# One bank pool, two operand buffers and wider products for a bidirectional recurrence

## The chip, the cores and the metric

The kernel runs on one core of a Trainium2 chip, in one launch. The metric is the device time of one execution in microseconds (us). Everything is computed in 32-bit floats. A 32-bit matrix product appears in the profile as two matmul records and two weight loads.

## The reference, cut to what matters

One layer with two parallel recurrent branches is followed by a mixture of experts. There are 256 context tokens and 256 latent tokens of width 1024.

```
u   = rmsnorm(h) * (1 + scale1) + shift1            # h: context, latent
p   = u @ w_in                                       # 6032 columns
yA  = gated_delta_net(p[A cols])                     # 4 heads x 128, chunks of 64, two directions
yB  = rwkv7(p[B cols])                               # 8 heads x 64, two directions
      # S_t = S_{t-1} (diag(w_t) + a_t b_t^T) + v_t k_t^T ;  y_t = S_t r_t
h  += gate1 * w_out(sig(p[gA]) * yA @ w_oA + sig(p[gB]) * yB @ w_oB)
h  += gate2 * moe(rmsnorm(h) * (1 + scale2) + shift2)    # 32 experts, two of them per token
out = rmsnorm(h)                                     # latent tokens only
```

Context tokens are needed for the recurrent states alone. The latent tokens of both branches start from the states that the context left.

## The kernel before

**Front.** `make_u` and `ada_first` compute the modulated input, which stays in SBUF as `u`. `proj` multiplies one 128-column tile of `w_in` with it: eight products of 128x128 weights into a PSUM tile `pj`, over 512 tokens (both streams) or over the 256 latent tokens. Most of TensorE's time goes there. `gate_cols` does the sixteen tiles of the two output gates and, after every second one, a piece of the modulation weights (`ada_rest`). These gate tiles need nothing but `u`, so they serve as filler.

**RWKV branch.** `rwkv_prep` makes the decayed operands of one segment (0 context, 1 latent) and one head pair p, sends them to DRAM (`rscr`), and computes the within-chunk products `ab` in the PSUM tile `abps`. `inverse` inverts the chunks' triangular matrices column by column on DVE (the pairs `itm`, `ixt`), and `inverse_join` joins the 32x32 halves on TensorE (`zps`). Then come four context steps (`R`) and four latent steps (`r`) of `rwkv_step`. One step loads X and A from DRAM (`rX`, `rA`), transposes the scaled keys (POOL `rKE`, PE `tmps`, ACT `rtm`) and the values (`vps`, `ruv`), makes the within-chunk products `akps` and masks them into `rak` and `rbk` (DVE), forms the right side `rps`, solves with the inverse (`ups`), updates the state (`sps`, `sbd`), and in a latent step writes the output (`yps`).

**GDN branch.** `gdn_cols`, `gdn_v`, `gdn_kk` and `gdn_kq` prepare keys, queries and values, a second `inverse` follows, and `gdn_step` runs eight steps: `gkt`, `gvt`, `gks`, `gup`, `gsp`, and for latent steps `gop` and `got`. `rwkv_post` and `merge_b`, `gdn_post` and `merge_a`, `out_rows` and `route` follow, then eight quads of four experts (`moe_quad`) that stream 100 MB of weights through six `wgu` and seven `wd` slots.

**Memory.** PSUM has eight banks of 128x512, dealt out by tag in `PSB` (L97): pp 1, sc 2 (one tile that spans both), pj 1, gc 2, ch 2. `sc` holds `abps`, `tmps`, `akps`, the joins' `zps` (except the last) and three tiles of `rwkv_post`; only one of these lives at a time. X has one buffer (`NB["rX"]`), so a step's load of X is issued after the last product of the step before has read it.

**Order.** The program is written as straight-line code. A planner simulates the engines and writes one fixed order of instructions for each engine and for each DMA queue: among the instructions that are ready by its own clock it takes the one of highest precedence. Precedence is the order of writing; `high_priority(n)` (in `hi`, L1517) moves a block n instructions ahead. In the string `go` of `NB` the parts between the two recurrences are written as `KGGgGGRRGRRikIVGQqJrrrrG`: K, Q, V are projections of the GDN branch, G a gate tile, R and r the recurrence steps, i and I inverses, J a join. R, i, I and J have 2000, V has -400, r has none. On the chip each engine executes its list strictly in order; SyncE (SP) issues nearly all DMAs, also in order. A pool (`w2`, twelve weight buffers) opens after the last latent step, in the space of the recurrence's operands, and the eight last gate tiles load through it.

Of the kernel before, what the change touches and what calls it, by code (L numbers as in the profile page):

```python
# [52 lines left out]
def constants():  # L53
# [21 lines left out]
    for d in range(2):  # L75
        mr[:, d] = (np.where(half == d, -1.0, 1.0)[:, None] * incl)[:, None]
# [20 lines left out]
PSB = {"pp": (1, 512), "sc": (1, 1024), "pj": (1, 512), "gc": (2, 512), "ch": (2, 512), "mx": (4, 512)}  # L97


class K:  # L100
# [64 lines left out]
    def psum(self, tag, name="ps"):  # L165
        b, w = PSB[tag]
        return (self.ps2 if tag in ("sc", "ch") else self.ps).tile([P, w], F32, tag=tag, bufs=b, name=name)
# [289 lines left out]
    def rwkv_prep(self, seg, p, B, ab, pool):  # L457
# [69 lines left out]
        m = self.cst("mka").unsqueeze(1).to_broadcast([P, 8, C])  # L527
        ps = self.psum("sc", name="abps")
        pv = ps.rearrange("p (e s j n) -> p e s j n", e=2, s=4, j=2)
        for e in range(2):  # L530
            r = slice(64 * e, 64 * e + 64)
            for s in range(4):
                for j in range(2):
                    for d in range(2):
                        self.mm(pv[64 * d:64 * d + 64, e, s, j, :], bks[d][r, s, j, d, :], acs[d][r, s, j, 0, :])
        for e in range(2):
            for s in range(4):
                self.tt(abv[:, e, s, 2 * p:2 * p + 2], pv[:, e, s], m[:, 0:2])
# [65 lines left out]
    def rwkv_step(self, seg, s, T):  # L604
        nc = self.nc
        x = lambda name, *dims, bufs=2: self.t(self.prt, name, *dims, bufs=bufs)
        X, A = self.t(self.prx, "rX", 1536, bufs=NB["rX"]), self.t(self.prx, "rA", 512 + 512 * seg, w=1024, bufs=2)
# [10 lines left out]
        if upd:  # L618
            KE = self.t(self.prx, "rKE", 2, 4, P, bufs=1)
            self.tt(KE, X[:, 0:1024].rearrange("p (d j n) -> p d j n", d=2, j=4), pc.to_broadcast([P, 2, 4, P]),  # L620
                    eng=nc.gpsimd)
            ps = self.psum("sc", name="tmps")
            for d in range(2):
                for j in range(4):
                    self.tr(ps[:, (4 * d + j) * P:(4 * d + j + 1) * P], KE[:, d, j])
            for d in range(2):
                self.act(tm[:, d, :], ps[:, d * 512:d * 512 + 512], scale=self.cst("sgn")[:, d:d + 1])
            if S is not None:
                Sp = self.t(self.pst, "rS", 2, 4, C, bufs=1)
# [9 lines left out]
        ak, rbk = x("rak", 2, 4, C), None  # L639
        if seg:  # L640
            rbk = [self.t(self.prx, "rbk", 2, 2, 2, C, bufs=NB["rbk"]) for _ in range(2)]
        for p in range(2):
            ps = self.psum("sc", name="akps")
            pv = ps.rearrange("p (e x) -> p e x", e=2)
            for e in range(2):
                r = slice(64 * e, 64 * e + 64)
                for j in range(2):
                    for d in range(2):
                        ko, uo = 64 * (1 - d), 64 * d
                        bk, a = BK[r, d, 2 * p + j], AR[r, d, 2 * p + j]  # L650
                        self.mm(pv[ko:ko + 64, e, j * C:(j + 1) * C], bk[:, 1 - d, :], a[:, 0, :])
                        if seg:
                            c0 = 128 + (2 * d + j) * C
                            self.mm(pv[ko:ko + 64, e, c0:c0 + C], bk[:, 1 - d, :], a[:, 1, :])
                            self.mm(pv[uo:uo + 64, e, c0:c0 + C], bk[:, d, :], a[:, 1, :])
            for e in range(2):
                self.tt(ak[:, e, 2 * p:2 * p + 2, :], pv[:, e, 0:128].rearrange("p (j n) -> p j n", n=C),
                        self.cst("mks").unsqueeze(1).to_broadcast([P, 2, C]))
            if seg:
                self.tt(rbk[p].rearrange("p e d j n -> p e (d j n)"), pv[:, :, 128:384],  # L660
                        self.cst("mkr").unsqueeze(1).to_broadcast([P, 2, 256]))
# [3 lines left out]
        for h in range(8):  # L665
            e, j = h % 2, h // 2
            for d in range(2):
                ur, kr = slice(64 * d, 64 * d + 64), slice(64 * (1 - d), 64 * (1 - d) + 64)
                self.mm(rv[ur, h, :], ak[kr, e, j, :], uv[kr, d, h * C:(h + 1) * C], start=S is None or h == 0,
                        stop=S is None)  # L670
# [31 lines left out]
        if seg:  # L702
            yp = self.psum("ch", name="yps")
            yv = yp.rearrange("p (d j n) -> p d j n", d=2, j=4)
            for h in range(8):
                e, j = h % 2, h // 2
                r = slice(64 * e, 64 * e + 64)
                for d in range(2):
                    o = yv[r, d, j, :]
                    self.mm(o, Sb[:, d, j, 64 * e:64 * e + 64], AR[:, d, j, 1, :], start=True, stop=False)  # L710
                    self.mm(o, uv[:, d, h * C:(h + 1) * C], rbk[j // 2][:, e, d, j % 2, :], start=False, stop=True)
# [9 lines left out]
    def rwkv_post(self, pool):  # L721
# [7 lines left out]
        for tgt in range(2):  # L729
            ps = self.psum("sc", name="mean")  # L730
            for i in range(2):
                self.mm(ps[:, i * 512:(i + 1) * 512], self.cst("bd"), f(yc if tgt else self.RY)[:, i * 512:(i + 1) * 512]
                        if tgt == 0 else f(sq)[:, i * 512:(i + 1) * 512])
            if tgt == 0:
                self.stt(f(yc), ps, -1.0 / 64, f(self.RY), ALU.mult, ALU.add)
                self.act(sq, yc, AF.Square)
            else:
                self.rsq(f(sq), ps, 64.0, 1)
# [3 lines left out]
        ps = self.psum("sc", name="gate")  # L742
        for j in range(4):
            self.mm(ps[:, j * L:(j + 1) * L], g2[:, j * P:(j + 1) * P], self.Bg)
        self.tt(yc, yc, ps.rearrange("p (j n) -> p j n", j=4))
# [229 lines left out]
    def gdn_step(self, s, T, tmp):  # L975
# [16 lines left out]
        ps = self.psum("pp", name="gvt")  # L992
# [36 lines left out]
        if lat:  # L1029
# [12 lines left out]
            ps = self.psum("pp", name="got")  # L1042
# [397 lines left out]
NB = {'st': 2, 'ys': 'PP', 'yc': [1, 1], 'hn': 'VAVA', 'im': 'AAPP', 'e': 7, 'rt': 13, 'w': 10, 'e1': 4, 'o2': 2, 'kvr': 2, 'cv': 'PVVPPVPPPVVV', 'g1': 3, 'g2': 0, 'imt': 1, 'gi': 0, 'hi': {'p00': 2500, 'p01': 2500, 'i0': 2500, 'gp': 2000, 'R': 2000, 'i': 2000, 'gs': 2000, 'I': 2000, 'J': 2000, 'p11': 200, 'j0': 1500, 'g': 400, 'V': -400, 'rw': 2000}, 'zf': 1, 'g0': 1, 'pe': 0, 'vr': 'vr', 'jt': 'pp', 'go': 'KGGgGGRRGRRikIVGQqJrrrrG', 'rX': 1, 'rbk': 2, 'ixt': 1, 'vh': 2, 'bk': 4, 'ar': 3, 'gm': 7, 'fp': [[28, 'pj'], [29, 'gc'], [20, 'gc'], [21, 'ch'], [22, 'ch']], 'at': ['pp', 'sc'], 'pf': {'ma': 2, 'oo': 0.5}, 'pm': 8, 'aa': 1, 'gr': 0, 'gu': ['pj', 'gc', 'gc'], 'gq': 2, 'gk': 2, 'w2': 12, 'ip': [0, 0, 4], 'gt': ['pj']}  # L1440
# [72 lines left out]
def build(tc, A, dbg=None, upto="all"):  # L1513
# [6 lines left out]
    with ExitStack() as ctx:  # L1520
# [7 lines left out]
        with ExitStack() as mix:  # L1528
# [4 lines left out]
            with ExitStack() as ph1:  # L1533
# [6 lines left out]
                with ExitStack() as s:  # L1540
# [27 lines left out]
                    with hi("j0"):  # L1568
                        k.inverse_join(ab[0], pinv, T0, t0, "sc")
# [24 lines left out]
                def inv1():  # L1594
                    t[1] = k.t(mp, "iT", 32, C)
                    x = k.inverse(ab[1], pinv, t[1], 1)
                    k.inverse_join(ab[1], pinv, t[1], x, "sc")
# [82 lines left out]
            for n, c, tag in (("gp", k.MID, "sc"), ("gq", k.OUT, "gc")):  # L1680
# [66 lines left out]
```

## Time and profile before

| | us |
|---|---|
| median of 3 runs | 889.32 (887.65 to 893.66) |
| the profiled execution | 891.71 |
| its span, first to last instruction | 889.9 |
| TensorE busy | 774.4 (87% of the span) |
| VectorE busy | 389.6 (44%) |
| mean granted TensorE clock | 0.917 of full speed |
| HBM read | 189.64 MB |

The span is what the trace covers; 1.8 us of the execution lie around it. PE is TensorE's matmuls, PEld its weight loads, DVE VectorE, ACT ScalarE, POOL GpSimd, SP SyncE. A granted clock of 1.0 is 2.4 GHz and 0.5 is 1.2 GHz; a value between them is a mean over a stretch. Busy time of matmuls is the union of records whose ends overlap the next one's start, so it is a guide to occupation and not to efficiency. The profile has one row per group of instructions with its busy time, its mean duration and the idle time in front of it. The rows used are quoted below.

### The profile page before, as it was taken

To read this page: it belongs to the slowest core of one execution; us is meant where nothing else is said; L and a number is where in the kernel's file an instruction comes from. 1 tells how busy PE (TensorE), PEld (TensorE's weight loads), DVE (VectorE), ACT (ScalarE), POOL (GpSimd) and SP (SyncE) were. 2 spreads that over 40 slices of the span, in tenths; PEclk is the share of its full clock that TensorE was granted. 3 is DMA by queue.
4 is the path that set the end of the run, shared out by engine and by line. 5 is a ranking of instruction groups with operands and counts; after the bars stand their busy time and mean duration, and the time that the engine had idled before them with its cause. 6 is when DMAs were issued, how large, how long until landed. Compare 5 with 4: busy or idle time off the path is not lost. (4 is left out here: it accounts for less than half of the span.)

```text
span 889.9 us, 15079 instructions
## 1 busy us (share of the span) xinstructions
PE 774.4 (87%) x6089; PEld 460.2 (52%) x6089; DVE 389.6 (44%) x799; ACT 228.7 (26%) x434; POOL 192.9 (22%) x279
## 2 busy tenths in 40 slices
PE   6999999896948899989889999969969996888785
PEld 1444657542535575576677766758445441333231
DVE  1324679999499343895234512233162210111012
ACT  0323554313544233246412231150030000000001
POOL 1013335355243153762401110000120000000000
PEclk8999899798868999999769999998989998899988
DMA  9831454454322963465463399987974999999993
GB/s 347 304 101 64 127 183 160 165 161 131 116 81 77 303 202 125 126 183 158 154 209 96 91 359 316 304 271 229 330 309 176 431 423 426 422 428 425 426 410 119
DMA packets 88361, 210.60 MB, mean 237 GB/s; under 512 B 7753, under 2 KB 37201, under 8 KB 80865
## 3 DMA queue, kind: packets, MB, share of 16 engines
q1 hardware_dynamic: 85248, 205.87, 63.7%
q10 hardware_dynamic: 3040, 3.74, 1.2%
q8 instruction: 49, 0.80, 0.4%
q14 instruction: 24, 0.19, 0.1%
HBM read 189.64 MB, written 19.94 MB: 235 GB/s over the span
## 5 line engine op out<-in xcount | busy, mean ns | idle before, releaser
L106 PE MATMUL pj<-u,w 128*128 128x256 f32 (+1 forms) x768 | 253.0, 484 | 5.5 <-DVE gz L119 2.6
L106 PEld LDWEIGHTS pj<-u,w 128*128 128x128 f32 x768 | 148.1, 198 | 96.7 <-issue 72.1
L106 PE MATMUL gup<-wgu,xs 128*32 128x512 f32 x512 | 79.1, 687 | 22.4 <-DMA wgu<-in_wgu_dram 22.3
L106 PEld LDWEIGHTS gup<-wgu,xs 128*32 128x32 f32 x512 | 19.9, 124 | 77.6 <-issue 45.6
L112 DVE TENSOR_TENSOR msg<-msg,gup 128x256 f32<-128x256 f32 x8 | 3.4, 422 | 120.8 <-ACT msg L122 120.8
L112 POOL TENSOR_TENSOR rl<-rl,mhalf 128x1 f32<-128x1 f32 x2 | 1.1, 548 | 226.7 <-DVE rl L116 226.7
L112 DVE TENSOR_TENSOR itm<-ixt,imt 128x31 f32<-128x31 f32 (+22 forms) x89 | 44.8, 503 | 4.3 <-POOL ixt L551 2.3
L106 PE MATMUL dnp<-wd,mhT 128*32 128x512 f32 x256 | 38.6, 598 | 4.1 <-DVE mhT L1343 4.1
L112 DVE TENSOR_TENSOR ixt<-ixt,itm 128x31 f32<-128x31 f32 (+22 forms) x89 | 40.8, 459 | 2.2
L122 ACT ACT_TABLE_LOAD x24 | 30.8, 1283 | 30.0 <-PE kkn L106 12.7
L106 PEld LDWEIGHTS xsp<-oh,h 128*128 128x128 f32 x256 | 32.6, 203 | 6.2 <-issue 6.2
L106 PE MATMUL xsp<-oh,h 128*128 128x128 f32 x256 | 34.0, 287 | 0.0
L112 POOL TENSOR_TENSOR cacc<-cacc,cm 128x512 f32<-128x512 f32 (+1 forms) x24 | 26.5, 1103 | 26.4 <-ACT cm L122 25.3
L122 ACT ACTIVATE msg<-gup 128x256 f32<-128x256 f32 x8 | 3.1, 383 | 112.4 <-PE gup L106 112.4
L106 PE MATMUL acc<-my,ohT 128*128 128x512 f32 x64 | 29.7, 596 | 0.0
L106 PE MATMUL acc<-w,m 128*128 128x512 f32 x64 | 28.3, 592 | 0.0
L122 ACT ACTIVATE xs<-xsp 128x512 f32<-128x512 f32 x8 | 4.8, 597 | 91.3 <-PE xsp L106 91.3
L112 POOL TENSOR_TENSOR shs<-xp 128x512 f32<-128x512 f32 (+1 forms) x15 | 13.4, 896 | 64.3 <-ACT xp L122 64.3
L112 POOL TENSOR_TENSOR h<-xres,rowscale 128x512 f32<-128x512 f32 x4 | 5.1, 1271 | 100.6 <-DVE xres L112 100.6
L112 POOL TENSOR_TENSOR gS<-gS,sdec 128x1024 f32<-128x1024 f32 x6 | 11.5, 1912 | 68.6 <-PE gop L106 39.7
L116 DVE TENSOR_SCALAR shtm<-pj,omu 128x256 f32<-128x256 f32 x25 | 12.0, 481 | 29.6 <-ACT xp L122 29.6
L106 PE MATMUL akps<-rA,rX 64*64 64x64 f32 x512 | 23.5, 245 | 1.4 <-ACT rtm L122 1.4
(374 smaller groups left out, 1265.4 us busy)
## 6 DMA issues: line engine op xcount, KB each, us to landing
wgu<-in_wgu_dram SPq DMA_DIRECT2D x28, 2048.0 KB
wd<-in_wd_dram SPq DMA_DIRECT2D x27, 1024.0 KB
w<-in_w_in_dram SPq DMA_DIRECT2D x96, 256.0 KB
w<-in_ada_w_dram SPq DMA_DIRECT2D x64, 256.0 KB
aw<-in_ada_w_dram SPq DMA_DIRECT2D x16, 512.0 KB
rX<-rscr SPq DMA_DIRECT2D x8, 768.0 KB
wgu<-in_wgu_dram SPq DMA_DIRECT2D x20, 256.0 KB
rscr<-bk SPq DMA_DIRECT2D x8, 512.0 KB
```

The source lines that it names most:

```text
L106: return self.nc.tensor.matmul(out, lhsT, rhs, start=start, stop=stop)
L112: (eng or self.nc.vector).tensor_tensor(out=out, in0=a, in1=b, op=op)
L116: (eng or self.nc.vector).tensor_scalar(out=out, in0=a, scalar1=s1, scalar2=s2, op0=op0, **kw)
L122: return self.nc.scalar.activation(out=out, in_=in_, func=func, **kw)
```

## The change

PSUM loses the tag `sc`. Its two banks go to `ch`, which now has four single banks for all these tiles; `gvt` and `got` of the GDN step move from `pp` to `ch` as well.

In `rwkv_prep` the `abps` products are written so that consecutive ones use the upper and lower half of the rows (e, in two banks) and both halves of the columns (d), and each bank is masked by one 128x512 operation in place of four of 128x128.

In a context step the sixteen products of both head pairs go into two banks and are masked by two operations in place of four. In a latent step a product takes both operands whole: 64 rows, 128 columns of weights, 128 moving columns. It replaces three of 64 by 64 (half of its upper output is not used), so 16 products stand for 48, and four masks of 128x512 stand for four of 128x128 and two of 128x512. The masked operands take eight buffers of 2 KB per partition (`arb`). X gets two buffers. Both together need 14 KB per partition more, net of `rak` and `rbk`. `rwkv_post` works in two halves.

The table of precedences gets `'r': 1000`: each latent step moves 1000 instructions ahead of where it is written, which is further than V, G, Q, q and J together are long. I and J keep their 2000. Nothing else of `NB` changes but the bank tag of `adat` (`'at'`: `['pp', 'ch']`).

```
     mr = np.zeros((P, 2, 2, 64))
     for d in range(2):
-        mr[:, d] = (np.where(half == d, -1.0, 1.0)[:, None] * incl)[:, None]
+        mr[:, d, 0] = strict
+        mr[:, d, 1] = np.where(half == d, -1.0, 1.0)[:, None] * incl
...
-PSB = {"pp": (1, 512), "sc": (1, 1024), "pj": (1, 512), "gc": (2, 512), "ch": (2, 512), "mx": (4, 512)}
+PSB = {"pp": (1, 512), "pj": (1, 512), "gc": (2, 512), "ch": (4, 512), "mx": (4, 512)}
...
-        return (self.ps2 if tag in ("sc", "ch") else self.ps).tile([P, w], F32, tag=tag, bufs=b, name=name)
+        return (self.ps2 if tag == "ch" else self.ps).tile([P, w], F32, tag=tag, bufs=b, name=name)
...
-        m = self.cst("mka").unsqueeze(1).to_broadcast([P, 8, C])
-        ps = self.psum("sc", name="abps")
-        pv = ps.rearrange("p (e s j n) -> p e s j n", e=2, s=4, j=2)
+        m = self.cst("mka").unsqueeze(1).unsqueeze(1).to_broadcast([P, 4, 2, C])
+        pvs = [self.psum("ch", name="abps").rearrange("p (s j n) -> p s j n", s=4, j=2) for _ in range(2)]
+        for s in range(4):
+            for j in range(2):
+                for d in range(2):
+                    for e in range(2):
+                        r = slice(64 * e, 64 * e + 64)
+                        self.mm(pvs[e][64 * d:64 * d + 64, s, j, :], bks[d][r, s, j, d, :], acs[d][r, s, j, 0, :])
         for e in range(2):
-            r = slice(64 * e, 64 * e + 64)
-            for s in range(4):
-                for j in range(2):
-                    for d in range(2):
-                        self.mm(pv[64 * d:64 * d + 64, e, s, j, :], bks[d][r, s, j, d, :], acs[d][r, s, j, 0, :])
-        for e in range(2):
-            for s in range(4):
-                self.tt(abv[:, e, s, 2 * p:2 * p + 2], pv[:, e, s], m[:, 0:2])
+            self.tt(abv[:, e, :, 2 * p:2 * p + 2], pvs[e], m)
...
-        X, A = self.t(self.prx, "rX", 1536, bufs=NB["rX"]), self.t(self.prx, "rA", 512 + 512 * seg, w=1024, bufs=2)
+        X, A = self.t(self.prx, "rX", 1536, bufs=2), self.t(self.prx, "rA", 512 + 512 * seg, w=1024, bufs=2)
...
-            ps = self.psum("sc", name="tmps")
             for d in range(2):
+                ps = self.psum("ch", name="tmps")
                 for j in range(4):
-                    self.tr(ps[:, (4 * d + j) * P:(4 * d + j + 1) * P], KE[:, d, j])
-            for d in range(2):
-                self.act(tm[:, d, :], ps[:, d * 512:d * 512 + 512], scale=self.cst("sgn")[:, d:d + 1])
+                    self.tr(ps[:, j * P:(j + 1) * P], KE[:, d, j])
+                self.act(tm[:, d, :], ps, scale=self.cst("sgn")[:, d:d + 1])
...
-        ak, rbk = x("rak", 2, 4, C), None
+
+        arb = lambda: self.t(self.prx, "arb", 512, bufs=8)
         if seg:
-            rbk = [self.t(self.prx, "rbk", 2, 2, 2, C, bufs=NB["rbk"]) for _ in range(2)]
-        for p in range(2):
-            ps = self.psum("sc", name="akps")
-            pv = ps.rearrange("p (e x) -> p e x", e=2)
+            m = self.cst("mkr").rearrange("p (d x) -> p d x", d=2).unsqueeze(2).to_broadcast([P, 2, 2, 2 * C])
+            rb = [[arb().rearrange("p (d j x) -> p d j x", d=2, j=2) for e in range(2)] for p in range(2)]
+            for p in range(2):
+                pvs = [self.psum("ch", name="akps").rearrange("p (d j x) -> p d j x", d=2, j=2) for e in range(2)]
+                for d in range(2):
+                    for j in range(2):
+                        for e in range(2):
+                            r = slice(64 * e, 64 * e + 64)
+                            self.mm(pvs[e][:, d, j], BK[r, d, 2 * p + j].rearrange("p a n -> p (a n)"),
+                                    AR[r, d, 2 * p + j].rearrange("p a n -> p (a n)"))
+                for e in range(2):
+                    self.tt(rb[p][e], pvs[e], m)
+            ak = lambda kr, e, d, j: rb[j // 2][e][kr, d, j % 2, 0:C]
+        else:
+            pvs = [self.psum("ch", name="akps")[:, 0:4 * C].rearrange("p (j n) -> p j n", n=C) for e in range(2)]
+            for j in range(4):
+                for d in range(2):
+                    ko = 64 * (1 - d)
+                    for e in range(2):
+                        r = slice(64 * e, 64 * e + 64)
+                        self.mm(pvs[e][ko:ko + 64, j, :], BK[r, d, j, 1 - d, :], AR[r, d, j, 0, :])
+            aks = [arb()[:, 0:4 * C].rearrange("p (j n) -> p j n", n=C) for e in range(2)]
             for e in range(2):
-                r = slice(64 * e, 64 * e + 64)
-                for j in range(2):
-                    for d in range(2):
-                        ko, uo = 64 * (1 - d), 64 * d
-                        bk, a = BK[r, d, 2 * p + j], AR[r, d, 2 * p + j]
-                        self.mm(pv[ko:ko + 64, e, j * C:(j + 1) * C], bk[:, 1 - d, :], a[:, 0, :])
-                        if seg:
-                            c0 = 128 + (2 * d + j) * C
-                            self.mm(pv[ko:ko + 64, e, c0:c0 + C], bk[:, 1 - d, :], a[:, 1, :])
-                            self.mm(pv[uo:uo + 64, e, c0:c0 + C], bk[:, d, :], a[:, 1, :])
-            for e in range(2):
-                self.tt(ak[:, e, 2 * p:2 * p + 2, :], pv[:, e, 0:128].rearrange("p (j n) -> p j n", n=C),
-                        self.cst("mks").unsqueeze(1).to_broadcast([P, 2, C]))
-            if seg:
-                self.tt(rbk[p].rearrange("p e d j n -> p e (d j n)"), pv[:, :, 128:384],
-                        self.cst("mkr").unsqueeze(1).to_broadcast([P, 2, 256]))
+                self.tt(aks[e], pvs[e], self.cst("mks").unsqueeze(1).to_broadcast([P, 4, C]))
+            ak = lambda kr, e, d, j: aks[e][kr, j, :]
...
-                self.mm(rv[ur, h, :], ak[kr, e, j, :], uv[kr, d, h * C:(h + 1) * C], start=S is None or h == 0,
+                self.mm(rv[ur, h, :], ak(kr, e, d, j), uv[kr, d, h * C:(h + 1) * C], start=S is None or h == 0,
...
-                    self.mm(o, uv[:, d, h * C:(h + 1) * C], rbk[j // 2][:, e, d, j % 2, :], start=False, stop=True)
+                    self.mm(o, uv[:, d, h * C:(h + 1) * C], rb[j // 2][e][:, d, j % 2, C:2 * C], start=False, stop=True)
...
-            ps = self.psum("sc", name="mean")
             for i in range(2):
-                self.mm(ps[:, i * 512:(i + 1) * 512], self.cst("bd"), f(yc if tgt else self.RY)[:, i * 512:(i + 1) * 512]
-                        if tgt == 0 else f(sq)[:, i * 512:(i + 1) * 512])
-            if tgt == 0:
-                self.stt(f(yc), ps, -1.0 / 64, f(self.RY), ALU.mult, ALU.add)
-                self.act(sq, yc, AF.Square)
-            else:
-                self.rsq(f(sq), ps, 64.0, 1)
+                h = slice(i * 512, (i + 1) * 512)
+                ps = self.psum("ch", name="mean")
+                self.mm(ps, self.cst("bd"), f(sq if tgt else self.RY)[:, h])
+                if tgt == 0:
+                    self.stt(f(yc)[:, h], ps, -1.0 / 64, f(self.RY)[:, h], ALU.mult, ALU.add)
+                    self.act(f(sq)[:, h], f(yc)[:, h], AF.Square)
+                else:
+                    self.act(f(sq)[:, h], ps, AF.Ln, scale=1.0 / 64, bias=self.eps[:, 1:2])
+        self.act(sq, sq, AF.Exp, scale=-0.5)
...
-        ps = self.psum("pp", name="gvt")
+        ps = self.psum("ch", name="gvt")
...
-            ps = self.psum("pp", name="got")
+            ps = self.psum("ch", name="got")
...
-                        k.inverse_join(ab[0], pinv, T0, t0, "sc")
+                        k.inverse_join(ab[0], pinv, T0, t0, "ch")
...
-            for n, c, tag in (("gp", k.MID, "sc"), ("gq", k.OUT, "gc")):
+            for n, c, tag in (("gp", k.MID, "ch"), ("gq", k.OUT, "gc")):
...
-NB = {... 'hi': {'p00': 2500, ... 'at': ['pp', 'sc'], ...}
+NB = {... 'hi': {'r': 1000, 'p00': 2500, ... 'at': ['pp', 'ch'], ...}
```

## Rows read from the trace of the kernel before

**Rows 1.** The page: busy time by engine, and TensorE's clock in 40 slices

```profile
PE 774.4 (87%) x6089; PEld 460.2 (52%) x6089; DVE 389.6 (44%) x799; ACT 228.7 (26%) x434; POOL 192.9 (22%) x279
PEclk8999899798868999999769999998989998899988
```

**Rows 2.** Stretches: length, busy time (instructions) by engine, clock, DMA share, GB/s

```profile
140.00:220.00 80.00, 65.76 (x316) 38.81 (x314) 77.36 (x136) 25.89 (x46) 37.01 (x39) 0.91 0.49 160
220.00:305.00 85.00, 63.07 (x793) 42.01 (x793) 59.74 (x110) 37.45 (x64) 30.60 (x32) 0.82 0.39 123
305.00:400.00 95.00, 91.86 (x994) 62.05 (x993) 59.09 (x116) 30.82 (x56) 50.33 (x95) 0.96 0.56 175
400.00:462.00 62.00, 54.00 (x847) 42.58 (x848) 22.37 (x42) 24.84 (x52) 16.94 (x24) 0.78 0.56 178
462.00:600.00 138.00, 129.02 (x1311) 96.14 (x1310) 46.70 (x102) 37.78 (x75) 12.55 (x8) 0.99 0.70 234
666.00:680.00 14.00, 13.06 (x98) 7.85 (x98) 2.56 (x9) 0.98 (x2) 0.00 (x0) 0.84 0.07 28
680.00:865.00 185.00, 153.26 (x934) 62.63 (x938) 27.66 (x64) 6.48 (x13) 0.00 (x0) 0.94 1.01 423
```

**Rows 3.** PE's waits from 205 to 310: total us, times, longest

```profile
PE zps L106 <- DVE imt L573: 8.7, 1, 8.7
PE rps L106 <- DVE rak L112: 6.9, 3, 3.5
PE tmps L109 <- POOL rKE L112: 4.6, 3, 2.3
PE sps L106 <- DVE ruv L684: 3.8, 1, 3.8
PE tmps L109 <- ACT iT L122: 1.9, 1, 1.9
PE akps L106 <- ACT rtm L122: 1.4, 1, 1.4
```

**Rows 4.** Timeline of PE, single bursts: start, us, what, shape, records

```profile
131.74 1.90 PE L106 MATMUL abps<-ar,bk 64*64 64x64 f32 x62
...
251.19 0.72 PE L106 MATMUL akps<-rA,rX 64*64 64x64 f32 x16
...
415.48 1.50 PE L106 MATMUL akps<-rA,rX 64*64 64x64 f32 x48
...
435.02 1.20 PE L106 MATMUL zps<-TG,ixt 32*32 32x32 f32 x64
...
477.14 1.16 PE L106 MATMUL gsp<-guu,gkd 64*128 64x128 f32 x16
```

**Rows 5.** DVE's groups of the masks, by shape: count, busy us, mean ns

```profile
L112 DVE TENSOR_TENSOR rak<-akps,cs 128x128 f32<-128x128 f32 x32 | 7.7, 281 | 1.0 <-PE akps L106 1.0
L112 DVE TENSOR_TENSOR ab<-abps,cs 128x128 f32<-128x128 f32 x32 | 6.9, 277 | 0.0
L112 DVE TENSOR_TENSOR rbk<-akps,cs 128x512 f32<-128x512 f32 x8 | 5.4, 680 | 2.0 <-PE yps L106 2.0
```

**Rows 6.** SP's waits over the span, two rows: total us, times, longest

```profile
SPq L608 <- PE akps L106: 29.5, 4, 16.6
...
SPq L345 <- PE yps L106: 4.3, 1, 4.3
```

**Rows 7.** Timeline: last join, first latent product, first and fifth gup

```profile
344.42 1.20 PE L106 MATMUL zps<-iT,ixt 32*32 32x32 f32 x64
...
366.69 0.79 PE L106 MATMUL akps<-rA,rX 64*64 64x64 f32 x18
...
464.66 0.76 PE L106 MATMUL gup<-gr,TG 64*64 64x128 f32 x10
...
503.04 0.44 PE L106 MATMUL gup<-gr,TG 64*64 64x128 f32 x4
```

**Rows 8.** Timeline of SP: the first weight loads after the last latent step

```profile
506.39 2.04 SPq L345 DMA_DIRECT2D w<-in_w_in_dram  x4
```

More of the change, by code (lines that the diff above doesn't have):

```diff
@@ L741, in rwkv_post @@
             self.stt(yc[:, j, :], yc[:, j, :], self.par("lb", j), bon[:, j, :], ALU.add, ALU.add)
[L742 to L745, printed above, removed]
+        for i in range(2):
+            ps = self.psum("ch", name="gate")
+            for j in range(2):
+                self.mm(ps[:, j * L:(j + 1) * L], g2[:, (2 * i + j) * P:(2 * i + j + 1) * P], self.Bg)
+            self.tt(f(yc)[:, i * 512:(i + 1) * 512], f(yc)[:, i * 512:(i + 1) * 512], ps)
         for j in range(4):
@@ L1439 @@
 PRE = (("wgu", 0), ("wgu", 1), ("wgu", 2), ("wd", 0), ("wgu", 3), ("wd", 1), ("wd", 2), ("wd", 3))
-NB = {'st': 2, 'ys': 'PP', 'yc': [1, 1], 'hn': 'VAVA', 'im': 'AAPP', 'e': 7, 'rt': 13, 'w': 10, 'e1': 4, 'o2': 2, 'kvr': 2, 'cv': 'PVVPPVPPPVVV', 'g1': 3, 'g2': 0, 'imt': 1, 'gi': 0, 'hi': {'p00': 2500, 'p01': 2500, 'i0': 2500, 'gp': 2000, 'R': 2000, 'i': 2000, 'gs': 2000, 'I': 2000, 'J': 2000, 'p11': 200, 'j0': 1500, 'g': 400, 'V': -400, 'rw': 2000}, 'zf': 1, 'g0': 1, 'pe': 0, 'vr': 'vr', 'jt': 'pp', 'go': 'KGGgGGRRGRRikIVGQqJrrrrG', 'rX': 1, 'rbk': 2, 'ixt': 1, 'vh': 2, 'bk': 4, 'ar': 3, 'gm': 7, 'fp': [[28, 'pj'], [29, 'gc'], [20, 'gc'], [21, 'ch'], [22, 'ch']], 'at': ['pp', 'sc'], 'pf': {'ma': 2, 'oo': 0.5}, 'pm': 8, 'aa': 1, 'gr': 0, 'gu': ['pj', 'gc', 'gc'], 'gq': 2, 'gk': 2, 'w2': 12, 'ip': [0, 0, 4], 'gt': ['pj']}
+NB = {'st': 2, 'ys': 'PP', 'yc': [1, 1], 'hn': 'VAVA', 'im': 'AAPP', 'e': 7, 'rt': 13, 'w': 10, 'e1': 4, 'o2': 2, 'kvr': 2, 'cv': 'PVVPPVPPPVVV', 'g1': 3, 'g2': 0, 'imt': 1, 'gi': 0, 'hi': {'r': 1000, 'p00': 2500, 'p01': 2500, 'i0': 2500, 'gp': 2000, 'R': 2000, 'i': 2000, 'gs': 2000, 'I': 2000, 'J': 2000, 'p11': 200, 'j0': 1500, 'g': 400, 'V': -400, 'rw': 2000}, 'zf': 1, 'g0': 1, 'pe': 0, 'vr': 'vr', 'jt': 'pp', 'go': 'KGGgGGRRGRRikIVGQqJrrrrG', 'rX': 1, 'rbk': 2, 'ixt': 1, 'vh': 2, 'bk': 4, 'ar': 3, 'gm': 7, 'fp': [[28, 'pj'], [29, 'gc'], [20, 'gc'], [21, 'ch'], [22, 'ch']], 'at': ['pp', 'ch'], 'pf': {'ma': 2, 'oo': 0.5}, 'pm': 8, 'aa': 1, 'gr': 0, 'gu': ['pj', 'gc', 'gc'], 'gq': 2, 'gk': 2, 'w2': 12, 'ip': [0, 0, 4], 'gt': ['pj']}
 def layout(inp):
@@ L1596, in inv1 @@
                     x = k.inverse(ab[1], pinv, t[1], 1)
-                    k.inverse_join(ab[1], pinv, t[1], x, "sc")
+                    k.inverse_join(ab[1], pinv, t[1], x, "ch")
                 def keys():
```

## The prediction

> **What bounds the kernel now.** I read the page first, then the kernel cut into stretches, then what PE waits for. PE is busy 87% of the span [rows 1], but that is an average over two regimes. From 680 to 865 us the DMA share is 1.01 at 423 GB/s, so there the experts' weights set the pace. Just ahead of it, from 666 to 680, the DMAs move 28 GB/s: all slots are full and the stream waits until the first quad frees one [rows 2]. So the end stands at a fixed distance behind the moment at which PE reaches that quad, and what is saved before it moves the end one for one, up to those 14 idle us and the slack that the prefetch has before them.
>
> Before 666 PE is the bound nearly everywhere: busy 92 of 95 us from 305 to 400 and 129 of 138 from 462 to 600. Three stretches are worse. From 140 to 220 DVE is busy 77 of 80. From 220 to 305 PE is busy 63 of 85 at a clock of 0.82. From 400 to 462 it is busy 54 of 62 at 0.78 [rows 2]. The second is the context recurrence, which shares DVE with an inverse; the third holds latent steps after dense projections have run out. A PE microsecond saved before 600 therefore counts, and an idle or half-clocked one that is filled counts too.
>
> **Part by part.** The sum runs against the profiled execution of 891.7 us (span 889.9); the median of the runs is 2.4 us lower, and the saving is taken off both.
>
> Latent products. Eight bursts of 48 records of 64 columns cost 1.50 us each (31 ns a record), 12.0 in all; in their place stand eight bursts of 16 records of 128 columns from 64 rows. That shape exists: `gsp`, also alternating between the two row halves, takes 1.16 us for 16 [rows 4]. That gives 8 x 0.34 = **2.7 saved**. Bounds: if the halves did not overlap, twice 1.16, a loss of 6.6; if a record cost the old 31 ns, 0.50 a burst, a gain of 8.0. I take the equal shape.
>
> Context products. Eight bursts of 16 at 0.72 become four of 32 in which neighbours use four different corners of the array. Unchanged rate would save nothing; the join's records, in neighbouring corners, run at 1.20/64 = 19 ns [rows 4], and at 19 for 31 the 128 records save 1.5. I take **1.2**. The same for `abps`: 256 records at 31 ns (62 in 1.90) to 19 is 3.1; bound 0; I take **2.5**, since not all will find a free neighbour.
>
> Masks on DVE. Thirty-two `ab` masks of 0.277, busy 6.9 in union, become eight of 128x512 at about 0.68, 5.4; a latent step goes from 4 x 0.28 + 2 x 0.68 = 2.5 to 4 x 0.68 = 2.7, a context step from 1.1 to less than 1.4 [rows 5]. Only the two `ab` preparations inside 140 to 220, where DVE is full [rows 2], count: half of 1.5, **0.7 saved**. The latent masks' extra 0.2 a step is nothing while projections cover it (DVE 22 of 62 busy there, [rows 2]); uncovered, 0.8.
>
> Waits of the context steps. PE lost 14.8 us to `rak` 6.9, `rKE` 4.6, `iT` 1.9 and `rtm` 1.4 [rows 3]. `rtm` and `iT` are waits for the one `sc` tile and go. A second X lets POOL scale the keys a step ahead, but POOL then has the convolution's sums in its list, so half of 4.6 goes. `rak` waits because DVE is inside the inverse; two operations per step instead of four save a second queueing, and I take 1.5 of 6.9. Together 7.1; as `ruv` at 3.8 is late next, and `imt` at 8.7 stays, I take **5**. Bounds 0 and 14.8.
>
> X's second buffer on SP's list. SP stood 29.5 us for a free X [rows 6], with weight loads queued behind. PE has no wait for those weights in the rows, so this is worth nothing by itself, beyond the keys above. The load is now issued a step earlier, past weight loads that are 0.3 us each to issue: nothing, covered by the twelve or ten weight buffers. The 14 KB cost nothing as long as the pools behind them wait for the same last latent step.
>
> Precedence of the latent steps. The first latent product ran at 366.7, 21 us after the last join of their inverse at 345.6, and the steps then took until 506, with Q, V and the second inverse ahead of them [rows 7, 8]. Moved forward they share PE with dense projections instead of following them. What it can give is the loss from 400 to 462: 8.0 us idle and 62 x 0.22 = 13.6 of clock [rows 2]. But the displaced projections do the same work elsewhere, and each step remains a chain over PE, ACT and DVE. Further, SP loads the last gate tiles only behind the last latent step (a wait of 4.3, [rows 6]), which now ends sooner and gives later stages filler. I take **5**, bounds -12 (the same loss a second time) and +20.
>
> Split halves in `rwkv_post`, `gvt` and `got` on other banks, and the joins' tiles: nothing, covered by projections on PE; the joins finish earlier but PE worked meanwhile.
>
> Sum: 2.7 + 1.2 + 2.5 + 0.7 + 5 + 5 = **17.1**: 874.6 for the profiled execution, **872** for the median.
>
> One thing is left out of the sum: the latent products now have another array shape (64x128) than `rps` and `ups` beside them (64x64). The rows price no such change alone; a burst's own tail can be had from them, since 48 records take 0.78 more than 16, so 0.72 holds 0.33 of tail [rows 4]. The Trainium skill, TensorEngine Tiling (Array Packing), Key Properties, says that changing the tiling mode drains TensorE: with one such tail for each of eight bursts, an estimate, the sum would be 14.5. No row here shows that.
>
> **Rivals.**
> (1) *Waits refill.* PE's work shrinks by 7.1 as above, but what is late next takes the place of every wait: DVE is in the inverse all the same, and the latent steps cannot start before 345.6 whatever their precedence, so that this part doesn't do what it says. For it: the order is made by a planner with its own clock, and `ruv` and `imt` were waits of the same size [rows 3]. Against: the `sc` waits have no heir. Time 889.3 - 7 = 882.
> (2) *Large gain.* The third stretch disappears (21 us) and most waits too (10): 889 - 7 - 31 = 851. Against it: above some 20 us the prefetch itself would be late, for DMAs are idle only in the 14 us before 680 and partly before that [rows 2].
> (3) *Slower: GDN steps without cover.* From 464.7 to 503.0 four steps of the other branch passed at 9.6 us each, interleaved with two latent steps, and PE was full at clock 0.99 [rows 2, 7]. A GDN step's own five bursts are at most 5 x 1.16 = 5.8 [rows 4]. If the latent steps are gone by then and the eight last gate tiles have not arrived or are used up, 3.8 us or more a step lie open, 30 over eight steps. Less the 17.1, this is 13 slower: 902. It decides from the point at which the filler ends before the fifth step.
> (4) *Slower: the clock.* The granted clock was 0.78 where short products of many banks followed one another, 0.96 to 0.99 beside dense projections [rows 2]. If with four banks in turn the stretch from 220 to 400 also ran at 0.78, it would lose 85 x 0.04 + 95 x 0.18 = 20; with 7.1 off, 902. The Trainium skill, TensorE: Matmul & The Clock Gate, A second HAM failure mode, says that cycling through banks each iteration leaves gaps between groups of matmuls in which the clock swings. The trace agrees for 400 to 462, where PE was busy only 54 of 62 us; but there waits for loads and small products came together, and I see no more gaps from more banks.
>
> **How the numbers follow.** The forecast (861 to 880) gets 0.47, (1) 0.23, (2) 0.13, (3) 0.12, (4) 0.05. A run-to-run spread of 0.7% makes 1% (880.4 to 898.2) the limit of what can be told from no change. Faster is the forecast and (2) with a little of (1)'s lower edge: 0.61. Same is the rest of (1), 0.22. Slower is (3) and (4): 0.17. The range goes from 853 to 899: it leaves out half of (2) and nearly all of (3) and (4), about 0.2.
>
> **What would show it.** Right: `akps` falls to 256 records, with latent bursts of 16 near 1.2 us; `abps` near 20 ns a record; no wait of `akps` for `rtm`; the last `yps` well before 506; the clock of the stretch before the last join at 0.9 or more; the first quad's `gup` about 17 us earlier and the experts' stretch as long as now. Wrong: PE's idle time between 220 and 305 unchanged with DVE as releaser (then it is (1)); gaps of 3 us or more in `gks` and `gup` after the last `yps` (3); half-clock stretches that grow (4); or the first quad earlier but the end not, with DMAs busy up to it.

## The result: 913.7 us, 2.9% slower, and the profile after

The changed kernel takes 913.67 us (median; 911.66 to 920.31) where the kernel before took 888.78 in the same comparison: ratio 1.0292, 95% interval 1.0231 to 1.0354. The prediction was 872, range 853 to 899. The profiled execution has a span of 912.9 us.

The page after, the two lines that answer to [rows 1]:

```profile
PE 783.3 (86%) x5833; PEld 462.4 (51%) x5833; DVE 381.2 (42%) x761; ACT 229.2 (25%) x436; POOL 196.0 (21%) x279
PEclk9999899988979999979999889887998998999988
```

The stretches after, columns as in [rows 2]:

```profile
140.00:220.00 80.00, 68.60 (x561) 43.20 (x560) 71.58 (x116) 34.18 (x57) 44.81 (x47) 0.87 0.50 164
220.00:305.00 85.00, 75.72 (x841) 49.05 (x841) 60.38 (x110) 37.16 (x65) 29.52 (x26) 0.92 0.56 186
305.00:400.00 95.00, 90.83 (x1089) 63.59 (x1086) 63.15 (x116) 29.90 (x50) 49.80 (x92) 0.98 0.32 100
400.00:462.00 62.00, 59.37 (x421) 41.93 (x420) 13.63 (x27) 18.77 (x40) 6.88 (x15) 0.92 0.67 237
462.00:600.00 138.00, 106.37 (x972) 79.16 (x967) 38.36 (x82) 29.46 (x68) 18.30 (x15) 0.89 0.58 197
666.00:680.00 14.00, 13.69 (x69) 8.70 (x67) 7.15 (x15) 5.15 (x11) 6.09 (x6) 1.00 0.87 356
680.00:865.00 185.00, 150.27 (x946) 64.24 (x946) 33.02 (x104) 8.56 (x17) 0.00 (x0) 0.92 0.93 390
```

Two stretches became what was hoped for. From 220 to 305 PE is busy 75.7 us at a clock of 0.92 (before 63.1 at 0.82), from 400 to 462 it is busy 59.4 at 0.92 (before 54.0 at 0.78). The loss lies behind them: from 462 to 600 PE is busy 106.4 of 138 at 0.89, where it was 129.0 at 0.99.

PE's waits over one us from 205 to 310, as in [rows 3]. Those for `rtm`, `iT` and `rKE` are gone:

```profile
PE rps L107 <- DVE arb L113: 5.6, 1, 5.6
PE ssq L107 <- ACT gsq L123: 2.1, 2, 1.1
PE vps L110 <- ACT ruv L123: 1.2, 1, 1.2
```

Where the time went is read by following the eight recurrence (GDN) steps, as in [rows 7]: the last join, the first `gvt`, the merge products `pab` on either side of it, and steps 1, 4 and 8:

```profile
481.14 1.20 PE L107 MATMUL zps<-TG,ixt 32*32 32x32 f32 x64
...
535.84 5.13 PE L107 MATMUL pab<-yc,w 128*128 128x256 f32 x23
540.80 1.04 PE L110 MATMUL gvt<-cs,gvc 128*128 128x128 f32 x8
541.67 3.19 PE L107 MATMUL pab<-yc,w 128*128 128x256 f32 x14
544.79 1.09 PE L107 MATMUL gup<-gr,TG 64*64 64x128 f32 x16
...
568.73 1.21 PE L107 MATMUL gup<-gr,TG 64*64 64x128 f32 x16 [0.51 <-DVE gr L120]
...
609.57 1.12 PE L107 MATMUL gup<-gr,TG 64*64 64x128 f32 x16 [1.80 <-DVE gr L120]
```

The first step's `gup` runs at 544.8 instead of 464.7, all eight steps pass behind the RWKV branch's merge, and PE waits inside them for DVE, for ACT and for the steps' own loads. What should have run beside them was used up earlier. Two stretches show it, columns as above, first of the kernel after (its third line is the part of the second from the first `gvt` on):

```profile
440.00:505.00 65.00, 56.58 (x536) 37.70 (x534) 10.58 (x21) 19.02 (x40) 9.45 (x14) 0.95 1.03 370
505.00:610.00 105.00, 75.82 (x636) 58.37 (x637) 35.77 (x81) 23.95 (x57) 12.61 (x8) 0.89 0.38 122
541.00:610.00 69.00, 48.73 (x518) 38.32 (x517) 22.74 (x54) 16.41 (x47) 11.47 (x6) 0.90 0.38 123
```

and of the kernel before:

```profile
440.00:505.00 65.00, 60.07 (x897) 48.92 (x898) 26.34 (x58) 14.18 (x36) 12.25 (x11) 0.87 0.43 137
505.00:610.00 105.00, 96.13 (x650) 70.33 (x651) 29.52 (x62) 27.55 (x48) 4.29 (x3) 0.95 0.87 296
```

After, the last gate and modulation tiles run from 440 to 505 and their weights fill the DMAs (1.03). From 505 to 610 the DMAs stand at 0.38 and PE is idle 29.2 us, against 8.9 before; 20.3 of the 29.2 lie behind the first `gvt` (from 541 on). The clock is lower too. From there the end is a fixed distance away: the span ends 303 us behind the eighth step's `gup` (912.9 - 609.6), before 300 (889.9 - 589.7). That distance lies between 298 and 303 us in every kernel below. So the question of all experiments was what holds the recurrence steps. A hold is meant here as a wait that the order, a bank or the memory puts on them beyond the data that they need.

### The profile page after: what moved, and what is told of

It reads as the page before. It is cut to its first block, busy times and chain, and to the rows that moved or that the text cites. A ratio compares the mean times of both kernels' runs of the same rounds, so it can differ in the third digit from the quotient of the medians.

```text
span 912.9 us, 14498 instructions
## 1 busy us (share of the span) xinstructions
PE 783.3 (86%) x5833; PEld 462.4 (51%) x5833; DVE 381.2 (42%) x761; ACT 229.2 (25%) x436; POOL 196.0 (21%) x279
## 5 line engine op out<-in xcount | busy, mean ns | idle before, releaser
L113 DVE TENSOR_TENSOR ixt<-ixt,itm 128x31 f32<-128x31 f32 (+22 forms) x89 | 45.8, 515 | 2.0
L113 DVE TENSOR_TENSOR itm<-ixt,imt 128x31 f32<-128x31 f32 (+22 forms) x89 | 37.9, 425 | 2.1
L123 ACT ACTIVATE xp<-pj 128x256 f32<-128x256 f32 x25 | 9.6, 385 | 70.3 <-PE pj L107 37.2
L107 PE MATMUL ada<-w,silc 128*32 128x512 f32 x128 | 25.0, 601 | 2.3 <-DMA w<-in_ada_w_dram 1.8
```

Of the source, the lines that this page charges most:

```text
L107: return self.nc.tensor.matmul(out, lhsT, rhs, start=start, stop=stop)
L113: (eng or self.nc.vector).tensor_tensor(out=out, in0=a, in1=b, op=op)
L123: return self.nc.scalar.activation(out=out, in_=in_, func=func, **kw)
```

## The experiments

The table has each run's median, its ratio to the kernel before with the interval, and from its trace the end of the last join, the issue of the first `gkc` load (the keys of the first recurrence step), and the start of the first and eighth `gup`. What each run changes is said below the table.

| run | us | ratio | join | gkc | gup 1 | gup 8 |
|---|---|---|---|---|---|---|
| before | 888.8 | | 439.4 | 443.6 | 464.7 | 589.7 |
| after | 913.7 | 1.029 [1.023, 1.035] | 482.3 | 491.9 | 544.8 | 609.6 |
| e1 | 912.8 | 1.025 [1.016, 1.033] | 438.2 | 462.6 | 547.9 | 611.1 |
| e2 | 898.6 | 1.012 [1.006, 1.018] | 444.0 | 460.8 | 487.2 | 594.0 |
| e3 | 919.5 | 1.034 [1.027, 1.040] | 388.5 | 465.1 | 552.4 | 613.5 |
| e4 | 909.4 | 1.024 [1.018, 1.030] | 483.8 | 494.2 | 511.8 | 603.1 |
| e5 | 893.7 | 1.005 [1.002, 1.007] | 442.2 | 464.7 | 470.7 | 593.2 |
| e6 | 926.3 | 1.039 [1.034, 1.045] | 444.4 | 446.0 | 561.3 | 624.2 |
| e7 | 902.8 | 1.015 [1.011, 1.019] | 444.6 | 467.3 | 486.8 | 602.4 |
| e8 | 869.2 | 0.976 [0.972, 0.980] | 421.5 | 426.5 | 440.6 | 569.1 |
| e9 | 904.3 | 1.016 [1.012, 1.021] | 417.2 | 472.4 | 487.5 | 603.3 |
| e10 | 897.0 | 1.010 [1.006, 1.014] | 442.6 | 441.5 | 467.7 | 593.1 |
| e11 | 884.8 | 0.994 [0.992, 0.997] | 442.3 | 442.4 | 462.9 | 587.1 |
| e12 | 885.0 | 0.997 [0.994, 1.000] | 442.3 | 445.5 | 463.0 | 583.8 |
| e13 | 883.3 | 0.996 [0.993, 1.000] | 436.0 | 436.9 | 460.5 | 581.0 |
| e14 | 876.6 | 0.989 [0.983, 0.995] | 422.2 | 426.2 | 447.1 | 573.7 |
| e15 | 910.4 | 1.024 [1.016, 1.031] | 473.5 | 493.2 | 513.6 | 610.1 |
| e16 | 900.7 | 1.016 [1.009, 1.023] | 446.6 | 447.4 | 468.2 | 594.2 |

**First round: which half of the change?** Theory A held that the precedence delays the steps, theory B that the banks and products do.

e1, the change without the precedence:

```diff
-NB = {... 'hi': {'r': 1000, 'p00': 2500, ...
+NB = {... 'hi': {'p00': 2500, ...
```

> The changed kernel with the one entry 'r': 1000 taken out of the precedences again. Theory A (the precedence: latent steps go ahead of the query projections, the join of the second inverse then waits for them, and the GDN steps end up alone behind used-up filler): last yps after 480 us, first gup before 480, time 868 to 889, under the kernel before. Theory B (the banks: four common banks, with gvt and got among them, hold the GDN steps up): gvt still late, time above 900.

e2, the precedence alone, in the kernel before:

```diff
-NB = {... 'hi': {'p00': 2500, ...
+NB = {... 'hi': {'r': 1000, 'p00': 2500, ...
```

> The kernel before with 'r': 1000 alone; banks, X buffer and products as before. Theory A: the GDN steps move late as in the changed kernel, first gup after 520 us, time 900 to 925. Theory B: no slowdown, 875 to 893.

e3, the change with the second inverse's join on `ch` instead of `pp`:

```diff
-'jt': 'pp'
+'jt': 'ch'
```

> The changed kernel with the join of the second inverse in the common banks (tag ch) in place of pp, which the query projections' sum of squares holds. Theory A with the bank as the link (the inverse is done near 391 us, the join waits until 461 for pp): zps of ML near 395 to 420, GDN steps begin 40 us or more sooner and overlap the gate tiles, time 875 to 895. Theory A without that link (steps wait for the projections or for their place in the order, whatever the bank): join earlier or not, time still 905 to 918. Theory B: 905 to 918.

e4, the change with two transposes of the recurrence back on `pp`:

```diff
-        ps = self.psum("ch", name="gvt")
+        ps = self.psum("pp", name="gvt")
...
-            ps = self.psum("ch", name="got")
+            ps = self.psum("pp", name="got")
```

> The changed kernel with gvt and got of the GDN step back in pp. Theory B (gvt at 540.8 us waits for a common bank behind merge_b): gvt within a few us of gkt near 500, time 885 to 900. Theory A: gvt moves forward at most to the end of the join at 482, steps still with little cover, time 900 to 916.

None of the undone parts brought the time back: 912.8, 919.5 (above every range given for it) and 909.4. Yet the precedence alone cost 10 us, between the two ranges of e2, so neither theory had it. The table's columns gave the clue. Without the precedence (e1) the join was back at 438 and the first `gup` still came at 548. With the join moved to another bank (e3) it ended 94 us earlier than in the changed kernel, and the first `gup` came later still. Something behind the join held, and one hold undone uncovers the next.

**Second round: two holds in series.** Theory C: `gvt` on `ch` is one of them.

e5 is e1 and e4 together.

> The changed kernel without the precedence of the latent steps and with the recurrence's gvt and got tiles back in bank pp; products, four ch banks and the second X buffer stay. Theory C: gvt in ch is what holds the recurrence steps: its buffer comes, in program order, behind the tiles of rwkv_post and merge_b, so the steps run after the last pab of merge_b (540 us and later in the changed kernel and in the one without precedence) with no work beside them; the precedence alone holds them too, through the late join (461-482 us). Each undone alone left the other in force (912.8 and 909.4). With both undone the first gup comes before 495 us and the time falls to 872-892. Theory D: the four shared banks and the new products themselves cost the time: 900 or more, first gup wherever it lies.

e6, in the kernel before only this:

```diff
-        ps = self.psum("pp", name="gvt")
+        ps = self.psum("ch", name="gvt")
...
-            ps = self.psum("pp", name="got")
+            ps = self.psum("ch", name="got")
```

> The kernel before with gvt and got moved to bank ch (two buffers of 512) and nothing else. Theory C: the first gvt waits for the pab tiles of merge_b, first gup after 535 us (before: 464.7), the eight steps run bare behind it, time 900-920. Theory D: no product and no bank count has changed, so 885-893.

e7 has the new products of `rwkv_prep` and `rwkv_step` with `arb` in the kernel before, both halves in one `sc` tile:

```diff
+            ps = self.psum("sc", name="akps")
+            pvs = [ps[:, 512 * e:512 * e + 512].rearrange("p (d j x) -> p d j x", d=2, j=2) for e in range(2)]
...
```

> The kernel before with the new products alone: abps interleaved over the row halves with merged masks, akps as 128x128 (latent) and interleaved 64x64 (context), all still in the one sc bank of 1024; no precedence, one X buffer, gvt and post as before. Theory C: the gain that was forecast for the products is real and shows when nothing holds the recurrence steps: 870-886. Theory D (the products cost more than they save, by their longer 105 ns records or by moved masks): 892 or more.

e8 has of these the `abps` part only, products and mask:

```diff
+        ps = self.psum("sc", name="abps")
+        pvs = [ps[:, 512 * e:512 * e + 512].rearrange("p (s j n) -> p s j n", s=4, j=2) for e in range(2)]
...
+            self.tt(abv[:, e, :, 2 * p:2 * p + 2], pvs[e], m)
```

> The kernel before with abps alone interleaved over the row halves and its masks merged from four to one per half. Both theories: the forecast's terms for it (2.5 us of TensorE and 0.7 us of VectorE) or part of them: 882-889; above 891 would speak against the products (Theory D).

Theory C held for e6: two names of a bank cost 37 us, 6 more than its range allowed. The timeline of PE in e6 shows the second `gvt` with PE idle 1.6 us for `tbs`, the result of the RWKV branch's merge:

```profile
555.64 3.05 PE L106 MATMUL pab<-yc,w 128*128 128x256 f32 x13
558.53 0.60 PE L109 MATMUL gvt<-cs,gvc 128*128 128x128 f32 x4
560.76 0.66 PE L109 MATMUL gvt<-cs,gvc 128*128 128x128 f32 x4 [1.63 <-DVE tbs L119]
```

In the program the steps stand behind the last gate tiles, `rwkv_post` and `merge_b`. The gate tiles and `merge_b` take tiles of `ch`, in the changed kernel `rwkv_post` as well. A tile with the same tag gets its buffer behind theirs, whatever precedence its step has. On `pp` nothing of theirs stands ahead. In e5 most came back, but 893.7 is 1.7 above its range, with the first `gkc` load at 464.7, just when the last latent step ended (its `yps` to 464.6). e8 gained 19.6 us where it was expected to give at most 7, and e7, with more of the new products, lost 14, as theory D had it.

**Third round: memory.** Theory E: the recurrence's buffers lie in the memory of the latent chain, and eight `arb` buffers of 2 KB in place of two `rak` and two `rbk` (8 KB per partition more) let them overlap with buffers that the last latent steps still use.

e9, in e8:

```diff
-'rbk': 2
+'rbk': 6
```

> The kernel before with abps interleaved (869.2 by itself) and rbk given six buffers in place of two: 8 KB more of the chain's memory per partition, as much as the eight arb buffers add, and no other change of work. Theory E: the recurrence's buffers (gkc and its like) lie where the latent chain's buffers lay, and with 8 KB more the first gkc load has to wait until latent steps have let them go: first gkc load after 460 us (426.5 by itself), first gup after 475, time 885-905. Rival F (what cost the time with the products is the products, and their longer records and masks): memory that is not used costs nothing, first gkc near 427 and 866-873.

e10, in e7 (and e11 the same in e5):

```diff
-        arb = lambda: self.t(self.prx, "arb", 512, bufs=8)
+        arb = lambda: self.t(self.prx, "arb", 512, bufs=4)
```

> The kernel with the new products alone in the one sc bank (902.8) with four arb buffers in place of eight, so that the chain's memory is that of the kernel before. Theory E: the first gkc load is free again, before 445 us (467.3 with eight), and the time falls to 862-882. Rival F: 895 or more, whatever the load does.

> The changed kernel without the precedence, gvt and got in bank pp (893.7 with eight arb buffers), and four arb buffers; four ch banks, the new products, two X buffers stay. Theory E: first gkc before 455 us (464.7 with eight), 868-886. Rival F: 890 or more.

e12, in e11:

```diff
-        X, A = self.t(self.prx, "rX", 1536, bufs=2), ...
+        X, A = self.t(self.prx, "rX", 1536, bufs=1), ...
```

> As the run before, with one X buffer: the four banks and the new products in the memory of the kernel before. Theory E: 866-886; against the run before it the second X buffer's worth, which the prediction put at up to 5 us. Against the products in the one sc bank with four arb buffers: the worth of four banks of 512 for one of 1024 and two of 512. Rival F: 890 or more.

e9 bears theory E out: 8 KB more for the same work cost 35 us. Its timeline shows the first load of the recurrence issued when the last `yps` ends (472.09 + 0.28), and so do those of e1, e3 and e5:

```profile
472.09 0.28 PE L106 MATMUL yps<-rbk,ruv 128*64 128x64 f32 x2
472.41 0.33 SPq L980 DMA_DIRECT2D gkc<-kscr  x1
```

With four `arb` buffers the load is free again in e10, e11 and e12 (441 to 446). With all three holds undone the banks and products stand at 884.8, 29 us under the changed kernel and 0.6%, 4 to 5 us, under the kernel before; without the precedence the prediction's sum had 12.1. e10 missed its range by 15 us: its load was free and its time still 28 us above e8, where rival F had it. So the products, or the plan that is made for them, cost time besides the memory. The second X buffer (e11 against e12) was worth nothing.

**Fourth round: the parts that were left.** e13 adds to e8 the context products, e14 the latent ones (four `arb` buffers), e16 the second X buffer (`'rX': 2`); e15 is e11 with the precedence back in (`'r': 1000`).

> The kernel before with abps interleaved (869.2 by itself) and, besides, the context steps' akps interleaved over the row halves in one go with one mask per half; latent products, banks and memory as before. Theory G: the merged context mask comes only after all sixteen products and late on VectorE (rps waited 7.1 us for it with the products alone, 4.4 us with abps alone), so 870-885. Theory H: it is the latent products that give the time back, and the context part gains its 1.2 us: 865-871.

> The kernel before with abps interleaved and, besides, the latent steps' products as 128x128 with four arb buffers (one sc bank); the context products stay as before. Theory H: 885-900, as with all products (897.0). Theory G: the latent part saves up to 2.7 us or costs up to 2, so 865-873.

> The changed kernel with gvt and got in bank pp and four arb buffers: of the three holds on the recurrence steps only the precedence is left (without it 884.8; with eight arb buffers 909.4). If the three holds are in series and the latest one decides, the precedence alone keeps the join at 460-485 and the time at 900-912. If each of them costs by itself, 890-899.

> The kernel before with abps interleaved and a second X buffer (6 KB more of chain memory, first gkc load not held by it in the planned order). If the X load was a wait worth up to 5 us, as the prediction had it: 863-868. If it was covered anyhow: 868-874.

e15 came as the series has it: the precedence alone, nothing else holding, costs 25.7 us. The last join, the last `qscr` store (output of the query projections) and the first `gkc` load in e15:

```profile
472.30 1.20 PE L107 MATMUL zps<-TG,ixt 32*32 32x32 f32 x64
482.10 0.61 SPq L793 DMA_DIRECT2D qscr<-o  x1
493.24 0.33 SPq L986 DMA_DIRECT2D gkc<-kscr  x1
```

and in e11 without the precedence:

```profile
438.13 0.36 SPq L793 DMA_DIRECT2D qscr<-o  x1
441.15 1.20 PE L107 MATMUL zps<-TG,ixt 32*32 32x32 f32 x64
442.41 0.43 SPq L986 DMA_DIRECT2D gkc<-kscr  x1
```

The join comes 31 us later, but the load comes 51 us later, 20 us behind the join, and in both kernels the first `gup` starts 20 us behind the load. So it is the load that counts here and not the join. In all kernels but those whose load waits for latent steps (e1, e3, e5, e7, e9) it is issued 2 to 11 us behind the last `qscr` store. So the precedence held the steps by way of the query projections that it displaced; what fills the 11 us in e15 is not shown.

e13 lost 14 us, as theory G had it, e14 lost 7.4, more than G and less than H allowed. e16 lost 31 where both of its expectations had a few us at most. Its `gkc` load was not held; its join was 25 us later than in e8, and so were the projections ahead of it. Why the plan puts them later is only partly seen (below); the rest is open.

e8 is the version that beats both kernels. Its second stretch shows where the gain begins, PE busy 71.7 at 0.89 against 63.1 at 0.82 in [rows 2]:

```profile
220.00:305.00 85.00, 71.67 (x833) 45.89 (x828) 57.88 (x115) 38.57 (x66) 32.10 (x28) 0.89 0.54 171
```

The recurrence's projections ran between the context steps and were through at 388 instead of 406. That the shorter products made room for them is shown by the order alone; no run separates the saved records from the plan that they brought about.

## Why the prediction was wrong, step by step

**Two steps failed, and either alone makes most of the loss.** The first is the zero in "Split halves in `rwkv_post`, `gvt` and `got` on other banks [...]: nothing". It cost 37 us alone (e6), and 19 on top of e5 (e1). The text asked whether the work was covered, not what stands ahead of a tile in its new tag. The second is the precedence, forecast at 5 gained: it costs 10 alone (e2) and 25.7 where it is the only hold (e15 against e11). With both in force, undoing one gives back 1 us (e1) or 4 (e4); with both undone 20 come back (e5), and 29 with the memory as well (e11).

**The memory** is a third zero. "The 14 KB cost nothing as long as the pools behind them wait for the same last latent step" failed in its condition: before, the first `gkc` load (443.6) did not wait for the last latent step, whose work ended at 506 [rows 8]. That could have been read from the trace: the first `gup` at 464.7 lies before the fourth latent step's end. The memory costs 35 us alone (e9) and 9 where the other two holds are undone (e5 against e11). In the changed kernel itself it held nothing: the latent steps end at 425 there, and with the precedence in force eight `arb` buffers stand at 909.4 (e4) and four at 910.4 (e15).

**Precedence.** The mechanism named was right in its first half: the steps did move, the last `yps` ended at 425 instead of 506, and the stretch 400 to 462 was filled. But what they displaced was not "the same work elsewhere". It was the Q and V projections, and the first load of the recurrence comes behind the last store of the Q projections; the recurrence sets the end. The join waited behind them only for its bank: moved to `ch` (e3) it ended at 388.5. The latent steps lead only to `rwkv_post` and `merge_b`, and ending them 81 us earlier brought the end no nearer.

**Rival (3), recurrence steps without cover**, had 0.12 and 902 us, and is what happened: steps without cover, with PE waiting inside them, and the gate tiles used up before. Its size differs: PE is idle 20.3 us from 541 to 610, 2.5 a step where the rival said 3.8, and another 8.9 from 505 to 541, ahead of the steps. The rival had its cause in the latent steps' early end alone; the holds were not in it, and so it was 12 us too low and far too unlikely. Rival (1) had the start wrong, for the first latent product ran at 314.8, and the waits: the six of [rows 3] come to 27.3 us, and after there are 8.9 in that stretch and 6.4 for `imt`, which now falls at 195, just ahead of it: 12.0 saved, where the sum had 5. (Rivals (1) and (4) also count 0.7 us of VectorE's masks in PE's 7.1; it is 6.4.) Rival (4) is not borne out: with four banks in turn the stretch 220 to 305 ran at 0.92, not 0.78.

**The terms.** `abps`: 62 records took 1.90 us, now 64 take 1.16. From start to start that is 30 ns a record before and 18 after (means over the records at full clock), 3.1 us for 256 records; the forecast was 2.5. Context products: 32 in 0.97 for twice 16 in 0.72, 1.9 over four steps, forecast 1.2. Latent products: forecast 1.16 us per burst of 16, which is right only where both halves stand together. Records of PE after, as in [rows 4]:

```profile
126.06 1.16 PE L107 MATMUL abps<-ar,bk 64*64 64x64 f32 x64
...
249.59 0.97 PE L107 MATMUL akps<-rA,rX 64*64 64x64 f32 x32
...
335.67 1.16 PE L107 MATMUL akps<-rA,rX 64*128 64x128 f32 x8
...
339.46 1.16 PE L107 MATMUL akps<-rA,rX 64*128 64x128 f32 x16
```

With a bank for each half the plan often took the eight records of one half as soon as its bank was free, in 1.16 us, and sixteen side by side took no longer. On average a record took 105 ns at full clock (from start to start), 13.4 us for all 128 against 12.0 before: 1.4 lost for 2.7 gained. In the one `sc` tile of e10 and e14 it was 71 and 66 ns, as the forecast's 1.16 for 16 has it, so the 7.4 us that e14 lost are not in these bursts. Masks: the `ab` group went from 6.9 to 5.1, as forecast, and the two `arb` groups take 13.9 where `rak` and `rbk` took 13.1 [rows 5]:

```profile
L113 DVE TENSOR_TENSOR arb<-akps,cs 128x512 f32<-128x512 f32 x16 | 10.7, 686 | 7.2 <-PE akps L107 7.2
L113 DVE TENSOR_TENSOR ab<-abps,cs 128x512 f32<-128x512 f32 x8 | 5.1, 679 | 0.0
L113 DVE TENSOR_TENSOR arb<-akps,cs 128x256 f32<-128x256 f32 x8 | 3.2, 415 | 0.0
```

In a context step "two operations instead of four save a second queueing" has the wrong sign in e13: the merged mask starts after all 16 products, and `rps` then waits for both. PE's waits in e13, and in e8 without it, as in [rows 3]:

```profile
PE rps L106 <- DVE rak L112: 8.4, 2, 7.3
```

```profile
PE rps L106 <- DVE rak L112: 5.2, 2, 4.4
```

These 3 us are a part of the 14 that e13 lost; the rest is open. In the changed kernel, with four banks, the wait fell from 6.9 to 5.6, about the 1.5 of the forecast.

The second X buffer on SP, forecast as nothing by itself and as part of the waits' 5 beyond, is nothing beside four banks (e11, e12) and 31 us lost beside e8.

**The sum as a method.** e8's two terms of the sum are 2.5 and 0.7 us and its gain is 19.6. Here the order is made anew for each version, and how it comes out moved the end by several times the records saved. A sum of records can't see that; e8 and e16 are one on each side. It also means that a difference of 7 to 14 us between two of these kernels (e2, e13, e14) can come from the plan as well as from the edit; for the holds the waiting load or tile is seen in the trace.

## What to carry to other kernels

Before counting records, find the chain that sets the end and follow its first instruction: a tile that it takes from a tag with other users, or a KB added to a pool whose memory it inherits, can become a wait on whatever stands ahead there, and precedence does not lift it. Give precedence to that chain, not to the one with slack, and price what it displaces by the chain that this feeds. Holds can lie in series: when undoing one part changes nothing, look at what moved in the trace before ruling the part out, and undo them together.

## What the runs showed of the hardware that was not expected

Short products of different array shapes that alternate on TensorE lost their speed here. In e16 the planner laid `sps` (128 rows) and the inverse's `zps` (32x32) in turn, two records each:

```profile
306.56 0.24 PE L106 MATMUL zps<-imt,ab 32*32 32x32 f32 x2
306.74 0.33 PE L106 MATMUL sps<-ruv,rtm 128*64 128x64 f32 x2
307.00 0.24 PE L106 MATMUL zps<-imt,ab 32*32 32x32 f32 x2
307.17 0.33 PE L106 MATMUL sps<-ruv,rtm 128*64 128x64 f32 x2
307.43 0.24 PE L106 MATMUL zps<-imt,ab 32*32 32x32 f32 x2
```

Four records take 0.43 us. By themselves two `sps` are 0.08 us (30 in 1.15 in e8's timeline, below) and two `zps` 0.04 (64 in 1.20 [rows 4]), so each change of shape costs an estimated 0.16 us at full clock. It went on from 305.7 to 313.7, 32 changes, some 5 us of the 31 that e16 lost (from 311.6 on the granted clock was 0.50).

```profile
309.05 1.15 PE L106 MATMUL sps<-ruv,rtm 128*64 128x64 f32 x30
```

Alternating by itself did not cost this. In the kernel before, pairs of `gup` follow each other at 0.11 us (ten records from 464.66 on, [rows 7]), and no slower with records of `akps`, also of the 64x64 shape, between them:

```profile
465.26 0.28 PE L106 MATMUL gup<-gr,TG 64*64 64x128 f32 x2
465.27 0.28 PE L106 MATMUL akps<-rA,rX 64*64 64x64 f32 x2
465.37 0.28 PE L106 MATMUL gup<-gr,TG 64*64 64x128 f32 x2
```

The Trainium skill, TensorEngine Tiling (Array Packing), Key Properties, says that a change of tiling mode drains TensorE; this stretch agrees, at 0.16 us a change. In the latent bursts, where the prediction had weighed the rule, no run prices the change of shape; the loss seen there is that of halves that did not run side by side.
